# Down's sums kept running in PSUM, leftover feature tiles ahead of Down, and x split inside Down's last chunk

## The chip, the cores and the metric

The kernel runs on one core of a Trainium2 chip. A core has TensorE for matmuls (results go to PSUM, 8 banks of 128 partitions x 512 numbers), VectorE (DVE) and ScalarE (ACT) for elementwise work, GpSimd (POOL) for elementwise work in SBUF, and SyncE (SP), which here issues the DMAs in one queue. The metric is the device time of one execution in microseconds.

## The reference

One decoder layer on x of 1024 tokens x 1024 channels in f32, pre-norm with residual adds:

```python
x = x + (sigmoid(g_a) * y_a W_a + sigmoid(g_b) * y_b W_b) @ W_out   # mixers
h = rms_norm(x, norm_ffn)
x = x + (silu(h @ w_gate) * (h @ w_up)) @ w_down                    # D_FF = 2816
gate = sigmoid(rms_norm(x, norm_ple) @ w_pg)
x = x + gate * (p @ w_pp)
out = rms_norm(x, norm_final)
```

The change lies in the product with `w_down`, called Down here, and in the gate with `w_pg` behind it (the embedding gate).

## The kernel before

Everything is held transposed: x as 8 tiles `x2[m]` of 128 channels x 1024 tokens, two token halves of 512. A matmul takes a 128 x 128 weight block and a 128 x 512 operand. For f32 accuracy each number is split into a rounded part and a rest: `split` (L104 to 106) writes the rounded part with ScalarE and the rest with VectorE (`whi` and `wlo` for weights, `t` for operands), `split_gain` (L109, 110) does so with a gain (`xsh`, `xsl`); `mm3` (L85 to 87) then needs three matmuls per block.

**Gate and Up** (L818 to 838) go over 11 pairs of feature tiles, i = 0 to 10. Each pair is computed by Strassen's seven products (`strassen`), running on in PSUM: bank `x` takes products 1, 3, 5 and 7, bank `y` the 4th and 6th, and ScalarE copies partial sums out on the way (L685). The result `ys`, four blocks of 128 x 512 (two feature tiles by two halves), is turned by `stage` into Down's seven operands (`b11` to `t4`, four POOL subtractions), split, and written to DRAM (`d_o[i]`, 512 KB each) during the next pair's Gate. The last pair, i = 10, is the leftover: its four blocks go to DRAM as they are (`d_l`, L838).

**Down** is Strassen again: a chunk c takes four feature tiles (pairs 2c and 2c + 1), of which there are five, and each chunk goes over four pairs of output tiles, mp. For each (c, mp), seven products of six matmuls (`product`, two feature blocks by three), 140 in all. The order of all engines in this loop is that of the program, written by hand (`manual_schedule`, L894); work from outside may be put in between. Each product has a PSUM bank of its own. After the following product is issued, VectorE adds the bank onto one of seven targets (`evacuate`, L880): three are parts of x, four are sums in SBUF, `u1, u5, u6, u7`, which in chunk 0 are filled by ScalarE copies instead (L878). In the last chunk, when an mp is done, `combine` (L889) adds these sums onto x: eight adds of 128 x 512 for each mp, on POOL and partly on VectorE.

The weights of a step are two raw pieces of 256 KB (`wraw`, six buffers). `prepare` makes four sums of half pieces on POOL (L860 to 863) and splits them with four buffers of `whi` and `wlo`, one step ahead. The operands of chunk c + 1 are loaded from DRAM (L149) while chunk c runs, 14 loads of 512 KB through a ring of 24 buffers (8 `tap`, 12 `tbp`, 4 `spare`); those of chunk 0 during the last Up. In the last chunk `d_l` is loaded and split into `act`.

**The leftover** follows (L946 to 959): for each of 8 output tiles and two halves, six matmuls, then VectorE adds the bank to x (L956), x is split with its gain (L109, 110), and its square (ScalarE, L598) is added to `acc` by POOL (L599).

**The embedding gate** (L988 to 1000) then makes, for each m, 24 matmuls of `w_pg` with the split x for the first half; `stat` turns `acc` into 1 / rms with small matmuls (L116) and a chain of small VectorE operations (L119 to 129), `spread` spreads it over partitions, `finish` applies it, the sigmoid and the embedding, and adds squares for the last norm on VectorE (L599). The second half follows, and the output.

Apart from the hand-written loops a planner orders the instructions of each engine ahead of time, by program order and by when it reckons that inputs and buffers are ready; each engine then works its list in order, and so does SP. A buffer is given anew once the last reader of its old tile is done.

## Time and profile before

| | us |
|---|---|
| median of 3 runs | 1478.54 |
| lowest, highest | 1475.67, 1483.15 |
| the profiled execution | 1479.81 |
| its span | 1477.6 |
| TensorE busy | 1425.9 (96%) |
| VectorE busy | 1018.9 (69%) |
| ScalarE busy | 640.4 (43%) |
| POOL busy | 450.6 (30%) |

Busy time counts instructions as long as they are in the engine; matmuls overlap, so a busy TensorE isn't one at its peak. `PEclk` is the granted clock of TensorE as a share of full speed. Up ends and Down begins about 1132 us into the span; the leftover part ends at about 1352, the embedding gate's last matmuls at about 1460.

### The profile page before, as it was taken

How to read it: one execution, taken by the hardware profiler on the slowest of the kernel's cores; microseconds unless marked ns; L12 is line 12 of the kernel's file. 1: busy time of each engine (PE TensorE's matmuls, PEld its weight loads, DVE VectorE, ACT ScalarE, POOL GpSimd, SP SyncE). 2: the span in 40 equal slices, each digit the busy share in tenths (PEclk: the TensorE clock that was granted, in tenths of full speed). 3: DMA queues.
4: the chain of work that ended last, by engine and by line, in shares of the span. 5: the costliest groups of instructions: out<-in, count | busy, mean ns of one | idle time of the engine just before them, and what ended most of it. 6: DMA issues, size and time to landing. Idle time of an engine off the chain costs nothing.

```text
span 1477.6 us, 19192 instructions
## 1 busy us (share of the span) xinstructions
PE 1425.9 (96%) x6538; PEld 1171.9 (79%) x6538; DVE 1018.9 (69%) x1556; ACT 640.4 (43%) x1190; POOL 450.6 (30%) x491
## 2 busy tenths in 40 slices
PE   8999999999999999998899999999999999987995
PEld 6888888888888878885688888888887888875885
DVE  7681268888787776579666666666664476799786
ACT  6131455555555543345344444444443322225443
POOL 5000012232223200015444444444433233379001
PEclk9999999999999999999899999999999999998998
DMA  5141875555442177332244443444457766511452
GB/s 200 57 133 39 270 214 157 143 150 150 139 112 93 43 248 264 108 115 94 93 143 156 157 155 138 157 150 152 153 208 300 268 251 253 195 49 53 135 180 69
DMA packets 102673, 226.98 MB, mean 154 GB/s; under 512 B 10928, under 2 KB 22704, under 8 KB 102576
## 3 DMA queue, kind: packets, MB, share of 16 engines
q1 hardware_dynamic: 102576, 225.77, 46.0%
q8 instruction: 51, 0.84, 0.2%
q14 instruction: 46, 0.38, 0.1%
HBM read 154.42 MB, written 71.30 MB: 153 GB/s over the span
## 4 chain that ended last, share of the span: by engine, by line
PE 80%; DVE 10%; issue 6%; POOL 1%; DMA 1%; ACT 1%; SPq 0%; POOLq 0%; DVEq 0%; ACTq 0%
PE mm L87 25%; PE mm L86 25%; PE mm L85 25%; DVE wlo L106 2%; DVE fail L411 1%; PE pt L429 1%; DVE t L106 1%; DVE xsl L110 1%; PE av L445 1%; PE av L444 1%; PE z L401 1%; PE z L402 1%; DVE ev L606 1%; DVE x L956 1%; PE mm L141 1%
## 5 line engine op out<-in xcount | busy, mean ns | idle before, releaser
L85 PE MATMUL mm<-t,whi 128*128 128x512 f32 x960 | 381.2, 397 | 9.8 <-ACT t L105 4.4
L105 ACT CAST whi<-wraw 128x512 fp32r<-128x512 f32 x336 | 206.2, 620 | 412.2 <-PE mm L86 245.0
L87 PE MATMUL mm<-t,wlo 128*128 128x512 f32 x960 | 379.4, 396 | 4.3 <-DVE wlo L106 4.3
L106 DVE TENSOR_TENSOR wlo<-wraw,whi 128x512 fp32r<-128x512 f32 x336 | 253.6, 760 | 188.1 <-ACT whi L105 181.3
L86 PE MATMUL mm<-t,whi 128*128 128x512 f32 x960 | 379.5, 395 | 3.8 <-DVE t L106 3.8
L85 PEld LDWEIGHTS mm<-t,whi 128*128 128x128 f32 x960 | 182.0, 190 | 55.6 <-ACT t L105 6.0
L87 PEld LDWEIGHTS mm<-t,wlo 128*128 128x128 f32 x960 | 181.8, 189 | 47.1 <-DVE wlo L106 6.1
L86 PEld LDWEIGHTS mm<-t,whi 128*128 128x128 f32 x960 | 182.2, 190 | 46.2 <-DVE t L106 5.3
L85 PE MATMUL mm<-xs,whi 128*128 128x512 f32 x384 | 154.6, 403 | 0.0
L87 PE MATMUL mm<-xs,wlo 128*128 128x512 f32 x384 | 150.4, 392 | 0.0
L86 PE MATMUL mm<-xs,whi 128*128 128x512 f32 x384 | 150.2, 391 | 0.0
L106 DVE TENSOR_TENSOR t<-ev,t 128x512 fp32r<-128x512 f32 x98 | 96.9, 1010 | 32.9 <-ACT t L105 32.6
L694 POOL TENSOR_TENSOR ws<-wraw 128x512 f32<-128x512 f32 x22 | 29.8, 1353 | 286.4 <-DVE wlo L106 138.6
L411 DVE TENSOR_TENSOR_SCAN fail<-fail 128x1024 f32<-128x1024 f32 (+3 forms) x64 | 87.3, 1365 | 27.3 <-POOL fail L409 26.9
L105 ACT CAST t<-ev 128x512 fp32r<-128x512 f32 x102 | 61.6, 620 | 82.0 <-DVE ev L739 37.7
L409 POOL TENSOR_SCALAR_AFFINE_SELECT fail<-fail 128x128 f32<-128x128 f32 x64 | 20.6, 322 | 226.6 <-ACT fail L407 201.1
L105 ACT CAST ath<-pt 128x256 fp32r<-128x256 f32 (+1 forms) x176 | 54.8, 335 | 69.5 <-PE pt L429 38.8
L87 PEld LDWEIGHTS mm<-xs,wlo 128*128 128x128 f32 x384 | 72.1, 188 | 15.8
L85 PEld LDWEIGHTS mm<-xs,whi 128*128 128x128 f32 x384 | 72.2, 188 | 11.8 <-ACT sg L373 0.2
L86 PEld LDWEIGHTS mm<-xs,whi 128*128 128x128 f32 x384 | 72.3, 188 | 11.6
L106 DVE TENSOR_TENSOR atl<-pt,ath 128x256 fp32r<-128x256 f32 (+1 forms) x176 | 61.3, 367 | 18.2 <-ACT ath L105 17.8
L410 POOL TENSOR_SCALAR_AFFINE_SELECT beta<-beta 128x128 f32<-128x128 f32 x64 | 66.6, 1041 | 22.5 <-ACT beta L408 21.5
(187 smaller groups left out, 2570.1 us busy)
## 6 DMA issues: line engine op xcount, KB each, us to landing
d_t<-t SPq DMA_DIRECT2D x40, 512.0 KB, 3.3
t<-d_t SPq DMA_DIRECT2D x40, 512.0 KB, 5.9
d_b<-t SPq DMA_DIRECT2D x30, 512.0 KB, 2.7
t<-d_b SPq DMA_DIRECT2D x30, 512.0 KB, 7.3
wraw<-in_w_gate SPq DMA_DIRECT2D x44, 256.0 KB, 2.8
wraw<-in_w_up SPq DMA_DIRECT2D x44, 256.0 KB, 3.0
wraw<-in_w_down SPq DMA_DIRECT2D x44, 256.0 KB, 5.1
wraw<-in_w_out SPq DMA_DIRECT2D x32, 256.0 KB, 3.3
```

The lines of the kernel that those rows point to most:

```text
L85: nc.tensor.matmul(ps, w[0], x[0], start=first, stop=False, skip_group_check=onto)
L86: nc.tensor.matmul(ps, w[0], x[1], start=False, stop=False, skip_group_check=onto)
L87: nc.tensor.matmul(ps, w[1], x[0], start=False, stop=last, skip_group_check=onto)
L105: nc.scalar.copy(hi, src)
L106: (eng or nc.vector).tensor_sub(lo, src, hi)
L110: nc.vector.scalar_tensor_tensor(lo, src, g, hi, ALU.mult, ALU.subtract)
L141: nc.tensor.matmul(ps, ones, diag, start=True, stop=True)
L401: nc.tensor.matmul(zo, q[:, base:base + P], kh[:, ks], start=True, stop=False)
L409: nc.gpsimd.affine_select(r[:, :P], r[:, :P], [[1, P]], ALU.is_gt, 1.0, base=0, channel_multiplier=-1)
L410: nc.gpsimd.affine_select(b[:, :P], b[:, :P], [[1, P]], ALU.is_gt, 0.0, base=0, channel_multiplier=-1)
L411: nc.vector.tensor_tensor_scan(r[:, :w], r[:, :w], r[:, :w], 1.0, ALU.mult, ALU.bypass)
L694: nc.gpsimd.tensor_add(s1, a21, a22)
```

## The change

Down's seven products are reordered (`t3` before `b22`), so that four of them run on in a bank that already holds an earlier sum. Two steps (output pairs) form a unit of 14 products that alternate between the pairs; each pair has banks `x`, `z` and `y`, used in the order x z x y x y x. After each product, VectorE adds the bank's present contents straight onto the part of x that this partial sum belongs to (`target`); the sums in SBUF and `combine` are gone. `Weights` holds the parts of `prepare`, spread over the slots of the unit before.

The leftover is now pair i = 0: its four blocks are split and stored during the next Gate (`plain_store`), loaded during the last Up (`plain_loading`), and multiplied between Up and Down, ahead of the loop. Chunk c takes pairs 2c + 1 and 2c + 2. The operands of the last pair, i = 10, aren't stored: `keep` splits them into SBUF (`last`), and the last chunk uses them from there. The ring is replaced by a list of homes for each chunk.

In the last chunk, a part of x that has had all its sums is split with its gain by `final`, at most one in a slot, into tiles in the place of `tbp` and `spare`. The squares of x move behind the first gate matmuls, on VectorE (`squares`); the embedding gate takes the second half of the tokens first, and its first three results wait in PSUM for the statistics.

```diff
@@ constants, scratch, staging @@
-DOWN = ("b11", "b21", "t2", "t1", "b22", "t3", "t4")
+DOWN = ("b11", "b21", "t2", "t1", "t3", "b22", "t4")
-    d_o = [{n: scr(f"d_{n}{i}", [P, S]) for n in DOWN} for i in range(FT // 2 - 1)]
-    d_l = [[scr(f"d_l{e}{h}", [P, HALF]) for h in range(2)] for e in range(2)]
+    d_o = {i: {n: scr(f"d_{n}{i}", [P, S]) for n in DOWN} for i in range(1, FT // 2 - 1)}
+    d_l = [[scr(f"d_l{e}{h}", [P, S]) for h in range(2)] for e in range(2)]
-    def store(dst, src):
+    def to_dram(dst, src):
     ...
+    def stage(ys, store):
     ...
@@ loads of operands @@
-    ring = {"at": 20}
-
-    def ring_pair():
-        i = ring["at"] % 24
-        ring["at"] += 1
-        return pair_tile(tap if i < 8 else tbp if i < 20 else spare)
+    homes = {0: [tbp] * 6 + [spare] * 4 + [tap] * 4, 1: [tap] * 4 + [tbp] * 10,
+             2: [tbp] * 2 + [spare] * 4 + [tap] * 8, 3: [tbp] * 12 + [spare] * 2, 4: [tap] * 7}
     ...
+        home = iter(homes[c])
         for n in DOWN:
-            o[n] = []
-            for k in range(2):
-                t = ring_pair()
-                move(t, d_o[2 * c + k][n])
-                o[n].append(sides(t))
+            o.setdefault(n, [])
+            for i in (2 * c + 1, 2 * c + 2):
+                if i < NF - 1:
+                    t = pair_tile(next(home))
+                    move(t, d_o[i][n])
+                    o[n].append(sides(t))
+                    yield
+
+    def plain_store(ys):
+        for (e, h), y in ys.items():
+            to_dram(d_l[e][h], y)
+            yield
+
+    plain = [[], []]
+
+    def plain_loading():
+        for e in range(2):
+            for h in range(2):
+                t = pair_tile(tap)
+                move(t, d_l[e][h])
+                plain[e].append(sides(t))
                 yield
+    ops = loading(0, op)
     ...
-        if i == NF - 1:
-            ops = loading(0, op)
-            for _ in range(4):
-                next(ops)
         ys = {}
+        early = plain_loading()
         for n, _ in enumerate(strassen([w_up[2 * i], w_up[2 * i + 1]], up_out(ys))):
-            if i == NF - 1 and n in (2, 3, 4, 5, 6):
-                next(ops)
-                next(ops)
-        if i < NF - 1:
-            staging = stage(i, ys)
-        else:
-            for (e, h), t in ys.items():
-                nc.sync.dma_start(d_l[e][h], t)
+            if i == NF - 1 and n > 0:
+                for _ in range(2):
+                    next(early if n < 3 else ops)
+        if i == 0:
+            staging = plain_store(ys)
+        elif i < NF - 1:
+            staging = stage(ys, lambda n, y, d=d_o[i]: to_dram(d[n], y))
@@ Down: kept operands, weights, leftover part @@
+    tb3x = ctx.enter_context(ExitStack())
+    tb3 = tb3x.enter_context(pool("tb3"))
+    wsp = tb3x.enter_context(pool("wsp", 2))
+    last = {}
+
+    def keep(n, y):
+        t = tb3.tile([P, S], F32R, name=f"k{n}")
+        split(*sides(t), y)
+        last[n] = sides(t)
+
+    staging = stage(ys, keep)
+    units = [(c, mpp) for c in range(NC) for mpp in range(KT // 4)]
     q = HALF // 2
     ...
+    class Weights:
     ...
+        def sums(self):
+            self.sx, self.s1 = ev(), ev(q)
+            s2, s4 = (self.sx.rearrange("p (k e d) -> p e k d", e=2, d=P)[:, e] for e in range(2))
+            s1 = self.s1.rearrange("p (k d) -> p k d", d=P)
+            nc.gpsimd.tensor_add(s1, self.a21, self.a22)
+            nc.gpsimd.tensor_sub(s2, s1, self.a11)
+            nc.gpsimd.tensor_sub(self.a21, self.a11, self.a21)
+            nc.gpsimd.tensor_sub(s4, self.a12, s2)
+
+        def both(self, n, m, w):
+            self.w[n], self.w[m] = (w, (0, 2)), (w, (1, 3))
+
+        def w1(self):
+            self.both(0, 1, halves(self.x))
+
+        def w2(self):
+            self.both(2, 5, halves(self.sx))
+
+        def ws(self):
+            pair = tuple(wsp.tile([P, q], F32R, name=n) for n in ("wsh", "wsl"))
+            split(*pair, self.s1)
+            self.w[3] = pair, (0, 1)
+
+        def w3(self):
+            self.both(4, 6, halves(self.y))
+
+    def target(mp, n):
+
+        e, h = ((0, 0), (0, 0), (0, 1), (1, 1), (1, 1), (0, 1), (1, 0))[n]
+        return 2 * mp + e, h
+
+    pair = [Weights(0, 0), Weights(0, 1)]
+    for w in pair:
+        for e in range(2):
+            w.load(e)
+    for m2 in range(KT // 2):
+        raw = fp.tile([P, HALF], F32, name="wraw", bufs=NRAW)
+        nc.sync.dma_start(raw.rearrange("p (m n) -> p m n", m=2),
+                          w_down[2 * m2:2 * m2 + 2, :, :2 * P].rearrange("m p n -> p m n"))
+        w = halves(raw)
+        if m2 > 1:
+            pair[m2 - 2].sums()
+        for e in range(2):
+            for h in range(2):
+                ps = bank()
+                for k in range(2):
+                    mm3(ps, col(w, 2 * e + k), plain[k][h], k == 0, k == 1)
+                xx = x2[2 * m2 + e][:, hs(h)]
+                nc.vector.tensor_add(xx, ps, xx)
+            next(staging, None)
+            if m2 > 0:
+                next(ops, None)
+    run(staging)
+    run(ops)
+    for w in pair:
+        w.w1()
+    pair[0].w2()
+    xs3 = []
+    fresh = []
+
+    def final(m, h):
+        split_gain(*part(xs3[m], hs(h)), x2[m][:, hs(h)], gain(2, m))
+
@@ Down: the units @@
+        def evacuate():
+            m, h, ps, done = waiting
+            xx = x2[m][:, hs(h)]
+            nc.vector.tensor_add(xx, ps, xx)
+            if done:
+                fresh.append((m, h))
+
+        for u, (c, mpp) in enumerate(units):
     ...
+                    tbx.close()
+                    sparex.close()
+                    xsp = ctx.enter_context(pool("xsp", side="right"))
+                    xs3 += [(xsp.tile([P, S], F32R, name=f"xsh{m}"), xsp.tile([P, S], F32R, name=f"xsl{m}"))
+                            for m in range(KT)]
+            ahead = [Weights(units[u + 1][0], 2 * units[u + 1][1] + i) for i in range(2)] if u + 1 < len(units) else None
+            steps = {0: [pair[1].w2], 1: [pair[0].ws], 2: [pair[1].ws], 3: [pair[0].w3], 4: [pair[1].w3]}
+            if ahead:
+                a, b = ahead
+                loads = {0: [(a, 0), (a, 1)], 1: [(b, 0)], 6: [(b, 1)]}
+                steps |= {7: [a.sums], 9: [b.sums], 11: [a.w1], 12: [b.w1], 13: [a.w2]}
+            else:
+                loads = {}
+            banks = [{}, {}]
+            for slot in range(14):
+                n, i = divmod(slot, 2)
+                for w, e in loads.get(slot, ()):
+                    w.load(e)
+                w, cols = pair[i].w[n]
+                name = "xzxyxyx"[n]
+                x = op[DOWN[n]] + ([last[DOWN[n]]] if c == NC - 1 else [])
+                ps = banks[i][name] = product(w, x, cols, banks[i].get(name))
                 if waiting:
-                    evacuate(*waiting)
-                waiting = i, n, ps
-                if n % 2 == 1 and mp < 3 or mp == 3 and n >= 1:
+                    evacuate()
+                waiting = *target(2 * mpp + i, n), ps, c == NC - 1 and n not in (0, 2, 3)
+                for step in steps.get(slot, ()):
+                    step()
+                if c == NC - 1 and fresh:
+                    final(*fresh.pop(0))
+                if mpp == 0 and slot % 2 == 1 and slot < 12 or mpp == 1 and slot % 2 == 1 or mpp == 1 and slot in (4, 8):
                     next(ops, None)
     ...
-    for _ in combine(KT // 2 - 1):
-        pass
     ...
+            pair = ahead
+        evacuate()
+        for x in fresh:
+            final(*x)
+    tb3x.close()
+    tapx.close()
     ...
@@ the embedding gate @@
+    def squares(h):
+        for m in range(KT):
+            square_into(acc, m, hs(h), nc.vector)
+
+    def spread_into(inv, sl, dg):
+        nc.scalar.copy(inv[:, sl], spread(psp, dg, (sl.stop - sl.start) // P))
+
+
+    held = []
     for m in range(KT):
         w = pieces(w_pg[m])
-        got = ple_gate(m, w, hs(0))
+        held.append((m, *ple_gate(m, w, hs(1))))
         if m == 0:
-            dgs = [stat(psp, acc[:, hs(i)], 4, ev()) for i in range(2)]
-            held = got
-            continue
-        if m == 1:
-            for i in range(2):
-                nc.scalar.copy(inv3[:, hs(i)], spread(psp, dgs[i], 4))
-            finish(0, *held, hs(0))
-        finish(m, *got, hs(0))
+            squares(1)
+        elif m == 1:
+            dg = stat(psp, acc[:, hs(1)], 4, ev())
+            squares(0)
+        elif m == 2:
+            spread_into(inv3, hs(1), dg)
+            dg = stat(psp, acc[:, hs(0)], 4, ev())
+        elif m == 3:
+            spread_into(inv3, hs(0), dg)
+        while m > 1 and held:
+            finish(*held.pop(0), hs(1))
+
     ...
```

## Rows read from the trace of the kernel before

**Rows 1.** Head of the page: span and instructions.

```profile
span 1477.6 us, 19192 instructions
```

**Rows 2.** Stretches: length, PE, PEld, DVE, ACT, POOL busy (count), PEclk, DMA share, GB/s.

```profile
1050.00:1097.00 47.00, 47.00 (x206) 38.16 (x205) 31.09 (x40) 22.00 (x40) 21.16 (x15) 1.00 0.43 157
...
1180.00:1220.00 40.00, 40.00 (x177) 32.95 (x176) 28.09 (x47) 9.30 (x17) 11.83 (x16) 1.00 0.66 239
...
1350.00:1360.00 10.00, 5.82 (x26) 4.40 (x24) 10.00 (x13) 7.79 (x13) 10.00 (x7) 1.00 0.00 0
```

**Rows 3.** Waits of TensorE from 1050: total us, times, longest.

```profile
PE mm L87 <- DVE wlo L106: 13.8, 3, 9.7
```

**Rows 4.** TensorE's timeline, last Up product: start, duration, what, idle before.

```profile
1115.20 0.80 PE L85 MATMUL mm<-t,whi 128*128 128x512 f32 x1 [3.20 <-ACT ev L685]
...
1118.29 0.40 PE L86 MATMUL mm<-t,whi 128*128 128x512 f32 x1
```

**Rows 5.** TensorE's timeline at the end of Down.

```profile
1321.44 0.50 PE L87 MATMUL mm<-t,wlo 128*128 128x512 f32 x1 [0.40 <-DVE wlo L106]
...
1328.20 0.80 PE L87 MATMUL mm<-t,wlo 128*128 128x512 f32 x1 [3.72 <-DVE wlo L106]
...
1333.38 0.40 PE L87 MATMUL mm<-t,wlo 128*128 128x512 f32 x1
```

**Rows 6.** TensorE's timeline at the start of the embedding gate.

```profile
1365.52 0.80 PE L87 MATMUL mm<-xsh,wlo 128*128 128x512 f32 x1 [9.70 <-DVE wlo L106]
...
1369.52 0.63 PE L87 MATMUL mm<-xsh,wlo 128*128 128x512 f32 x1
1369.95 2.25 PE L116 MATMUL mm<-ones,acc 128*128 128x1 f32 x16
```

**Rows 7.** Groups of instructions from 1132 to 1365: count, busy us, mean ns, idle before.

```profile
L889 POOL TENSOR_TENSOR x<-x,s 128x512 f32<-128x512 f32 x15 | 23.3, 1565 | 3.0 <-DVE x L889 1.3 <-DVE x L880 1.2
...
L861 POOL TENSOR_TENSOR wraw<-wraw 128x256 f32<-128x256 f32 x19 | 14.7, 771 | 1.5
```

**Rows 8.** Tile x on VectorE, 1130 to 1365: ns min/median/max, first and last start.

```profile
L880 DVE TENSOR_TENSOR x<-mm,x x60: 674/681/685, 1135.0 to 1333.1; 128x512 f32<-128x512 f32 x60
L956 DVE TENSOR_TENSOR x<-mm,x x16: 675/678/683, 1334.8 to 1362.0; 128x512 f32<-128x512 f32 x16
L110 DVE SCALAR_TENSOR_TENSOR xsl<-x,g_sb,xsh x15: 750/1182/1778, 1336.3 to 1362.6; 128x512 fp32r<-128x512 f32 x15
```

**Rows 9.** VectorE's timeline, end of Down and first statistics.

```profile
1333.13 0.68 DVE L880 TENSOR_TENSOR x<-mm,x 128x512 f32<-128x512 f32 x1
...
1334.83 1.28 DVE L956 TENSOR_TENSOR x<-mm,x 128x512 f32<-128x512 f32 x2
...
1371.34 0.16 DVE L119 TENSOR_SCALAR nrm_a<-mm 128x4 f32<-128x4 f32 x1 [2.39 <-PE mm L116]
...
1376.30 0.87 DVE L129 TENSOR_SCALAR ev<-ident,nrm_y 128x128 f32<-128x128 f32 x4
```

**Rows 10.** Tile wlo on VectorE, 1130 to 1365: ns min/median/max.

```profile
L106 DVE TENSOR_TENSOR wlo<-wraw,whi x64: 681/693/1777, 1131.3 to 1363.7; 128x512 fp32r<-128x512 f32 x64
```

**Rows 11.** Timeline of SP's queue, last Up: start, us at it, DMA, count.

```profile
1097.73 3.09 SPq L149 DMA_DIRECT2D t<-d_b  x4
1100.87 0.67 SPq L535 DMA_DIRECT2D wraw<-in_w_up  x1
...
1118.57 11.32 SPq L838 DMA_DIRECT2D d_l<-ev  x3
```

**Rows 12.** Tile wraw on SP, 1130 to 1320: from issue to landing.

```profile
DMA to landing us min/median/max: 2.5/4.7/9.6
```

**Rows 13.** Group of the page: split of an operand on VectorE.

```profile
L106 DVE TENSOR_TENSOR t<-ev,t 128x512 fp32r<-128x512 f32 x98 | 96.9, 1010 | 32.9 <-ACT t L105 32.6
```

**Rows 14.** Tile acc, 1330 to 1470: squares added on VectorE, ns min/median/max.

```profile
L599 DVE TENSOR_TENSOR acc<-acc,ev x16: 418/684/693, 1385.7 to 1462.8; 128x512 f32<-128x512 f32 x12, 128x256 f32<-128x256 f32 x4
```

**Rows 15.** Stretch of the first gates, columns as in rows 2.

```profile
1378.00:1421.00 43.00, 43.00 (x192) 35.13 (x191) 32.48 (x54) 21.26 (x35) 0.00 (x0) 1.00 0.45 141
```

More of the change, by code (lines that the diff above doesn't have):

```diff
@@ L901, in hybrid_block @@
                 if c == NC - 1:
-                    act = [operand(tap, 2) for _ in range(2)]
-            if i + 1 < len(order):
-                ahead = prepare(raws.pop(i + 1))
-            for n, name in enumerate(DOWN):
-                if n == 0 and i + 2 < len(order):
-                    raws[i + 2] = load(i + 2)
-                if i + 1 < len(order) and n in (1, 2, 5, 6):
-                    w_next = next(ahead)
-                ps = product(w[n][0], op[name], w[n][1])
-                if waiting:
-                    evacuate(*waiting)
-                waiting = i, n, ps
-                if n % 2 == 1 and mp < 3 or mp == 3 and n >= 1:
-                    next(ops, None)
-                if c == NC - 1:
-                    if mp == 0:
-                        if n < 4:
-                            t = ev()
-                            nc.sync.dma_start(t, d_l[n // 2][n % 2])
-                            split(*act[n // 2][n % 2], t)
-                    else:
-                        if n == 0:
-                            comb = combine(mp - 1)
-                        next(comb, None)
@@ L926, in hybrid_block @@
-            for _ in comb:
-                pass
-            if c < NC - 1 and mp == 3:
+                    tbx.close()
[4 more added lines that the diff above has]
+            ahead = [Weights(units[u + 1][0], 2 * units[u + 1][1] + i) for i in range(2)] if u + 1 < len(units) else None
@@ L929, in hybrid_block @@
+            if c < NC - 1 and mpp == 1:
                 run(ops)
                 op = nxt
-            w = w_next
-        evacuate(*waiting)
-    for _ in combine(KT // 2 - 1):
-        pass
-    tbx.close()
-    sparex.close()
-    accx.close()
-    xsp = ctx.enter_context(pool("xsp", side="right"))
-    xs3 = [(xsp.tile([P, S], F32R, name=f"xsh{m}"), xsp.tile([P, S], F32R, name=f"xsl{m}")) for m in range(KT)]
+            pair = ahead
+        evacuate()
+        for x in fresh:
+            final(*x)
@@ L942, in hybrid_block @@
+    tb3x.close()
+    tapx.close()
     pp = ctx.enter_context(pool("ple"))
     acc = pp.tile([P, S], F32, name="acc")
-    for c in range(KT // 2):
-        raw = fp.tile([P, HALF], F32, name="wraw", bufs=NRAW)
-        nc.sync.dma_start(raw.rearrange("p (m n) -> p m n", m=2),
-                          w_down[2 * c:2 * c + 2, :, 4 * NC * P:].rearrange("m p n -> p m n"))
-        w = halves(raw)
-        for e in range(2):
-            for h in range(2):
-                m = 2 * c + e
-                ps = bank()
-                for k in range(2):
-                    mm3(ps, col(w, 2 * e + k), act[k][h], k == 0, k == 1)
-                xx = x2[m][:, hs(h)]
-                nc.vector.tensor_add(xx, ps, xx)
-                split_gain(*part(xs3[m], hs(h)), xx, gain(2, m))
-                square_into(acc, m, hs(h), nc.gpsimd)
```

90 lines of the change are left out of this document (27 added, 63 removed).

## The prediction

> **What bounds the kernel now.** The page's head gives the span, 1477.6 us [rows 1]; the execution it was taken from took 1479.8 us, 2.2 of them outside the span, and the median of the three runs, 1478.5, is 1.3 below it. I work against 1479.8 and subtract 1.3 at the end.
>
> I read the table by stretch first. In Up (1050 to 1097) and in mid Down (1180 to 1220) TensorE is busy all the time at the full clock; VectorE, in mid Down, 28.1 of 40 us: TensorE is the bound, with room on VectorE. From 1350 to 1360 that is turned round: VectorE and POOL 10.0 of 10.0, TensorE 5.8 [rows 2]. The waits of TensorE after 1050 then say what its idle time waited for: 13.8 us in 3 waits for `wlo`, a VectorE split, the longest 9.7 [rows 3]. TensorE's own timeline shows what each costs. A matmul follows the last after 0.23 us at the full clock, and after 0.43 for a while behind each long gap (the lower level of the clock).
> - Front, in the last Up product: 3.20 us idle; 7 matmuls then take 3.09 instead of 1.61, 1.5 lost: **4.7** [rows 4].
> - End of Down: 0.40 and 3.72 idle; 12 matmuls then take 5.2 instead of 2.8: **6.5** [rows 5].
> - Just inside the embedding gate: 9.70 idle; 9 matmuls then take 4.0 instead of 2.1: **11.6** [rows 6].
>
> Together 22.8 us of TensorE time in the stretch that the change rewrites.
>
> **The change part by part.**
>
> *TensorE's work* stays: 140 products of 6 matmuls and 96 for the leftover tiles in both versions. A product is 6 x 0.23 = 1.38 us, a unit of 14 products 19.3 us, the leftover part 22.1 us. So nothing is to be won in the middle of Down, only in the losses above.
>
> *Sums in PSUM.* 32 combining adds in the last chunk go: 23 on POOL (15 of them 1565 ns each [rows 7]), 9 on VectorE. ScalarE's 16 copies of the first chunk become VectorE adds, so VectorE has 140 evacuations instead of 124. One takes 681 ns, and they start 0.60 apart (two in 1.28) [rows 8, 9]. Per unit VectorE has 14 x 0.60, six full splits at about 0.61 and two half ones at 0.34: 12.8 of 19.3 us. The 16 new ones are among the 28 of the first chunk's two units, which keep 6.5 us free each: nothing. What replaces the separate banks is a wait: a product that runs on in a bank may not start until VectorE has read it. Queued behind the waiting matmul is all of TensorE. The two pairs put three products, 4.1 us, between a bank's end and its next use; VectorE needs 0.68 plus at most one split ahead of it, 1.78 at the longest [rows 10]. I take 0; it becomes a cost once VectorE runs more than 4.1 us late. It has done so: counted back from the gate's start at about 1352, the 96 leftover matmuls with 6.1 us lost among them began at about 1324, so the last Strassen product's evacuation, at 1333.13 [rows 9], was some 9 us late. That late in the new loop would be 5 us of waiting.
>
> *Leftover tiles first.* They leave the end, where each of the 16 results needed an evacuation, a gained split and mostly a POOL add, and go between Up and Down. What stalled the front goes with the order of loads: before, four 512 KB operand loads stand on SP at 1097.73, ahead of the next weights, and the stores of the last Up hold SP for 11.3 us further on [rows 11]. After, the Up weights come first, the operand loads start from the second product on, and those stores don't exist (the last stage's operands stay in SBUF), so the leftover part's weights can land during the last Up product: 4.7 us in the middle, 9.6 at most [rows 12]. I take the front's 4.7 as gone. What is late next there is VectorE: 16 evacuations (9.6), four splits of weights and three for the first unit (7 x 1.1, between the median and the longest of [rows 10], as POOL works beside them) and seven kept splits at 0.99 [rows 13] are 24.2 us against 22.1. Least cost 0, since the kept splits have until the last chunk; most, at 1.78 for all 14 splits, 34.5 - 22.1 = 12.4, and 2.0 for the clock behind it (as in the bullets), 14.4. I take 2.1, by the middle of the rows.
>
> *x split in the last chunk.* 16 gained splits move from behind Down into its last two units. They took 1182 ns in the median, with POOL at work, and 750 at the least [rows 8]; 0.67 apart in the second case, with the same 0.08 of overlap as above. In the first of the two units (POOL adds weights in it, 8 x 0.77 [rows 7]) VectorE has 14 evacuations, 8 splits of x, six full and two half splits of weights. At the slow durations that is 8.4 + 9.4 + 6.6 + 1.0 = 25.4, 6.1 over the 19.3, and 8.1 with the clock; at the fast ones 8.4 + 5.4 + 3.7 + 0.7 = 18.2, no stall. In the second unit POOL has no work: 8.4 + 5.4 + 2.5 + 1.2 for the gate's first weights = 17.5. I take 1.0, near the fast end, as POOL works only 6 us of the 38.6. The evacuations are 674 to 685 ns throughout [rows 8], a split with both inputs in SBUF 681 to 1777 [rows 10].
>
> The Trainium skill ("SBUF — State Buffer", Who interferes with whom) states that a VectorE instruction with two SBUF inputs contends with a GpSimd instruction that reads SBUF, and that one with at most one such input does not. By that rule the second unit has no slow split, and the chunk costs what 6 us of POOL cause, about 1 us; without it, by the median of the old splits, 8.1. The trace agrees: the evacuations don't vary, the splits do.
>
> *The gate after Down.* TensorE can go on at once, since the gate's first half needs nothing of the last product. What moves there is the sum of squares: 14 adds, from POOL at the end of Down to VectorE between the gates (684 ns, 0.60 apart: 8.4 us) [rows 14]. From 1378 to 1421 VectorE was busy 32.5 of 43.0 us [rows 15]; for the eight gates of 44 us that is 33.3. With two statistics of together 5.9 us (1371.34 to 1377.2 [rows 9]) it is 33.3 + 8.4 + 5.9 = 47.6, against TensorE's 44 and 2.3 of small matmuls [rows 6]. The squares stand ahead of the splits of the next weights, which TensorE waits for. Least 0; most the 8.4 in full with 2.0 of clock, 10.4. I take 3.0: the 1.3 of excess, and as much again since it comes in the first gates. The results held back occupy three of eight banks, which costs nothing.
>
> *Loads.* As many chunk loads of 512 KB less seven, into chosen homes. I walked each: the tightest are those of the sixth operand, issued behind products 7 and 8 of a chunk's second unit into tiles last read by its products 0 and 1. Over 8 us lie between: 0.
>
> Sum: 22.8 - 2.1 - 1.0 - 3.0 = 16.7. 1479.8 - 16.7 - 1.3 = 1461.8, forecast **1462** (1457 to 1468 for errors of the three costs).
>
> **The rivals.**
> - *All is hidden*: the three costs are 0: 1479.8 - 22.8 - 1.3 = 1455.7. For it: 0.40 us of waiting left the clock alone [rows 5], and most waits have slack. Against: VectorE's sums come out over the limit in two places.
> - *VectorE stays the bound at the end*: the last chunk at its 8.1 and half of the gate's 10.4: 22.8 - 2.1 - 8.1 - 5.2 = 7.4 gained, 1471. For it: the 10.0 of 10.0 there now, and that the work is the same but for the adds. Against: POOL, which stretched the splits, is nearly idle in the new end.
> - *The stall moves to the start of Down*: the front at its 14.4, the rest as forecast: 22.8 - 14.4 - 4.0 = 4.4, 1474. The leftover part would be as VectorE-bound in its new place as in the old.
> - *SP is held by an operand load* (slower): a load whose home tile is still read stops the weight loads queued behind it on SP, as the stores held it for 11.3 us [rows 11]. The last weight of a unit is issued at product 6 and its sum is split at 14: 11.0 us, of which landing takes 4.7 and POOL's four adds 3.1, so 3.2 are spare; 8.1 late and 2.0 of clock are 10.1 for each such chunk. From three of the four chunk changes on it outweighs the gain: 1492 to 1502. Against it is the walk above.
> - *Waits one by one* (the change doesn't do what it says): each of the 80 products that run on in a bank waits 0.1 us for its evacuation: 8 us, 1470. Against it: Gate and Up run on in PSUM too, with one other product between, and mid Up shows none [rows 2].
>
> The Trainium skill ("PSUM — Partial Sum Buffer", PSUM bank collisions raise a hardware error) asks that a bank be guarded by semaphore whatever address in it is read. By that the wait is there for each of those products and none can be left out; it would give 1470 if VectorE just misses each, and the forecast if it is never late. Mid Up, guarded in the same way, agrees with the second.
>
> **How the numbers follow.** Forecast 0.56, all hidden 0.13, VectorE-bound end 0.16, front 0.06, SP held 0.05, one by one 0.04. A measurement of this kernel can tell about 0.5% from no change, 7.4 us: faster ends at 1471.1, slower begins at 1485.9. Faster: 0.56 + 0.13 + half of 0.16 + 0.01 of the front + 0.02 of the waits = 0.80. Slower: the 0.05 of SP. Same: 0.15. The range takes in 1455.7 and the two waits' cases, with 2.7 below for the estimate of the losses: 1453 to 1473; outside lie SP, the upper part of the front and of the VectorE case, and a little below, some 0.16.
>
> **What would show it.** Right: no wait of 3 us on TensorE between 1097 and the end of Down; the leftover's matmuls directly behind Up; evacuations at 0.68; splits of x at 0.75 in the last unit; the gate's first matmuls within 1 us of the last product, and its start some 15 to 20 us earlier. Wrong: waits of TensorE for an evacuation of x inside Down (bank), for `wlo` in the first unit (front) or in gates 2 to 6 (squares), or SP entries of many us in Down. A time above 1473 means that VectorE or SP took the place of the stall; one below 1453, that I missed a loss.

## The result, and the profile after

The changed kernel takes 1468.68 us in the median of six runs (1465.48 to 1471.42), the kernel before 1483.26 beside it (1475.67 to 1484.08): a ratio of 0.991, 95% interval 0.9892 to 0.9928, so 10.7 to 16.0 us faster. On another chip, later, it was 0.9897 (0.9875 to 0.9918). The forecast was 1462, worked out from a kernel before at 1478.5, the median of its first three runs. Against the 16.7 us of its sum the gain is real and some 2 to 5 us short: 14.6 between the medians, 11.6 between the two profiled executions, 1479.81 and 1468.20, in which the terms can be followed.

Head of the page, then stretches (PE, PEld, DVE, ACT and POOL busy, PEclk, DMA share, GB/s), of the kernel after:

```profile
span 1466.5 us, 19073 instructions
```

```profile
1110.00:1120.00 10.00, 10.00 (x45) 8.20 (x44) 3.39 (x5) 2.94 (x5) 2.59 (x3) 1.00 1.01 388
1120.00:1130.00 10.00, 7.00 (x30) 5.09 (x29) 7.30 (x9) 2.18 (x4) 5.29 (x5) 1.00 0.77 292
1130.00:1140.00 10.00, 10.00 (x39) 7.96 (x38) 9.94 (x13) 4.04 (x7) 4.67 (x4) 0.83 0.56 185
1160.00:1200.00 40.00, 40.00 (x175) 32.50 (x173) 28.88 (x45) 8.70 (x16) 12.36 (x18) 1.00 0.66 247
...
1330.00:1340.00 10.00, 8.41 (x36) 6.26 (x35) 9.42 (x17) 3.81 (x7) 0.00 (x0) 1.00 0.17 52
...
1350.00:1360.00 10.00, 9.63 (x47) 7.84 (x46) 9.52 (x17) 6.34 (x12) 0.00 (x0) 1.00 0.50 173
1360.00:1370.00 10.00, 7.55 (x32) 5.72 (x32) 8.47 (x24) 4.33 (x9) 0.00 (x0) 0.95 0.14 45
1370.00:1380.00 10.00, 10.00 (x32) 7.78 (x33) 6.38 (x22) 4.00 (x6) 0.00 (x0) 0.71 0.21 63
```

The middle of Down is as it was: TensorE 40.00 of 40, VectorE 28.88 (28.09 in [rows 2]). What differs is at three seams, and each has a smaller wait where a larger one was, or one where none was. Waits of TensorE after, from 1050 (total us, times, longest), against the 13.8 us for `wlo` of [rows 3]:

```profile
PE mm L141 <- DVE ev L129: 5.8, 3, 4.9
PE mm L116 <- DVE acc L600: 5.3, 3, 2.5
PE mm L87 <- DVE wlo L106: 1.8, 1, 1.8
PE mm L85 <- DVE x L949: 1.6, 2, 1.2
PE mm L85 <- ACT whi L105: 1.2, 1, 1.2
```

L949 is the evacuation inside Down (L880 before), L600 the add of a square. The 4.9 (4.7 before) and one 2.5 belong to the end of the kernel and are in both versions.

**Front.** TensorE's timeline (start, duration, what, idle before):

```profile
1126.07 0.50 PE L85 MATMUL mm<-t,whi 128*128 128x512 f32 x1 [1.23 <-ACT whi L105]
...
1129.05 0.50 PE L87 MATMUL mm<-t,wlo 128*128 128x512 f32 x1 [1.78 <-DVE wlo L106]
```

Behind the second wait the matmuls come 0.43 apart instead of 0.23 until 1133.5, with the granted clock at 0.83 in that slice. Why the weights are late is seen on SP (start, us at it, DMA, count) and in the landing of its `wraw` loads, 1095 to 1125:

```profile
1107.26 0.33 SPq L535 DMA_DIRECT2D wraw<-in_w_down  x1
1107.69 1.81 SPq L149 DMA_DIRECT2D t<-d_l  x4
1111.79 2.43 SPq L149 DMA_DIRECT2D t<-d_b  x4
1114.51 1.00 SPq L149 DMA_DIRECT2D t<-d_t  x2
1115.60 0.38 SPq L535 DMA_DIRECT2D wraw<-in_w_down  x1
1116.14 1.67 SPq L917 DMA_DIRECT2D wraw<-in_w_down  x2
```

```profile
DMA to landing us min/median/max: 2.6/6.2/9.1
```

The leftover's first weights (L917) are issued at 1116.14, behind ten operand loads of 512 KB (5.2 MB, 13.5 us at the 388 GB/s of 1110 to 1120). With 9.1 us to landing that is 1125.2, when Up's last matmuls are done (TensorE is idle until 1126.07). ScalarE and VectorE (timelines of each) then show a second queue:

```profile
1124.88 0.62 ACT L105 CAST kb<-ev 128x512 fp32r<-128x512 f32 x1 [7.01 <-PE mm L87]
1125.40 0.61 ACT L105 CAST whi<-wraw 128x512 fp32r<-128x512 f32 x1
```

```profile
1125.49 2.38 DVE L106 TENSOR_TENSOR kb<-ev,kb 128x512 fp32r<-128x512 f32 x2
1127.79 1.21 DVE L106 TENSOR_TENSOR wlo<-wraw,whi 128x512 fp32r<-128x512 f32 x1
```

Two kept splits (`kb`) stand ahead of the weights' rest `wlo` in VectorE's list. The first wait, for `whi`, is thus mostly the late landing; the second, for `wlo`, has these two splits in it as well.

**End of Down.** TensorE, with the gate's first matmul last:

```profile
1332.81 0.47 PE L85 MATMUL mm<-t,whi 128*128 128x512 f32 x1 [1.22 <-DVE x L949]
...
1338.97 0.47 PE L85 MATMUL mm<-t,whi 128*128 128x512 f32 x1 [0.37 <-DVE x L949]
...
1347.41 0.39 PE L85 MATMUL mm<-xsh,whi 128*128 128x512 f32 x1
```

Evacuations over Down and splits of `x` on VectorE (ns min/median/max), against [rows 8], and VectorE's timeline ahead of the longer wait:

```profile
L949 DVE TENSOR_TENSOR x<-mm,x x138: 676/692/693, 1153.7 to 1348.0; 128x512 f32<-128x512 f32 x138
...
L110 DVE SCALAR_TENSOR_TENSOR xsl<-x,g_sb,xsh x13: 739/752/753, 1312.4 to 1347.3; 128x512 fp32r<-128x512 f32 x13
its engine sat idle before it (us, times) until:
...
  ACT xsh L109: 3.8, 10
```

```profile
1331.31 0.75 DVE L110 SCALAR_TENSOR_TENSOR xsl<-x,g_sb,xsh 128x512 fp32r<-128x512 f32 x1 [0.19 <-ACT xsh L109]
1331.98 0.68 DVE L949 TENSOR_TENSOR x<-mm,x 128x512 f32<-128x512 f32 x1
```

The bank comes free when the evacuation of 1331.98 ends. VectorE reached it late, having waited ten times, 3.8 us in all, for ScalarE's rounded part `xsh` of the split just ahead: seven times about 0.2 us, and 0.79 in each of three where nothing stood between the evacuation and the split of the same part.

**Gate.** TensorE, then VectorE:

```profile
1368.83 1.76 PE L116 MATMUL mm<-ones,acc 128*128 128x1 f32 x8 [2.45 <-DVE acc L600]
1370.45 0.77 PE L85 MATMUL mm<-xsh,whi 128*128 128x512 f32 x1
```

```profile
1362.90 4.67 DVE L600 TENSOR_TENSOR acc<-acc,ev 128x512 f32<-128x512 f32 x6
1367.49 0.68 DVE L106 TENSOR_TENSOR wlo<-wraw,whi 128x512 fp32r<-128x512 f32 x1
1368.09 0.68 DVE L600 TENSOR_TENSOR acc<-acc,ev 128x512 f32<-128x512 f32 x1
```

The first half's statistics stand in TensorE's list ahead of the fourth result and wait for the last square; the 12 matmuls behind come 0.43 apart.

**The ledger.** From TensorE's timeline I sum, over each stretch, how far the distance between starts goes beyond 0.23 us per matmul. The gate's column holds some 2.8 us of small matmuls and short gaps that every version keeps.

| us lost | front | end of Down | first gates |
|---|---|---|---|
| before | 4.8 | 7.0 | 13.0 |
| after | 5.1 | 2.1 | 7.8 |
| after, second chip | 3.9 | 2.0 | 6.9 |

That is 24.8 before and 15.0 after: 9.8 of the 11.6 us. Some 0.9 of the rest is there before 1085 us, in code that the change doesn't touch, and 0.5 lies outside the two spans, which are 11.1 apart. The gate's column is the least exact: from the gate's first matmul to the spread of the last norm's first half (L141 at 1424.54 before, 1413.64 after) it is 72.1 us before and 66.2 after, 5.9 less where the ledger has 5.2; and by the same count the changed kernel takes 64.7 on the second chip. Differences of under some 1.5 us in this column, between executions on different chips, tell nothing.

What went is thus the end of Down and part of the gate; the front's loss has only changed its cause. No run separates the leftover's move from the sums in PSUM.

### The profile page after: what moved, and what is told of

It is laid out like the page before. It is cut to its first block, busy times and chain, and to the rows that moved or that the text cites. A ratio compares the mean times of both kernels' runs of the same rounds, so it can differ in the third digit from the quotient of the medians.

```text
span 1466.5 us, 19073 instructions
## 1 busy us (share of the span) xinstructions
PE 1424.5 (97%) x6538; PEld 1170.6 (80%) x6538; DVE 1021.8 (70%) x1577; ACT 630.6 (43%) x1174; POOL 393.2 (27%) x454
## 4 chain that ended last, share of the span: by engine, by line
PE 82%; DVE 8%; issue 6%; DMA 1%; POOL 1%; ACT 1%; SPq 0%; DVEq 0%; POOLq 0%; ACTq 0%
PE mm L87 25%; PE mm L86 25%; PE mm L85 25%; DVE fail L411 1%; PE pt L429 1%; DVE t L106 1%; DMA xt<-in_xT 1%; DVE wlo L106 1%; PE av L445 1%; PE av L444 1%; PE z L401 1%; PE z L402 1%; DVE ev L607 1%; PE mm L116 0%; PE mm L141 0%
## 5 line engine op out<-in xcount | busy, mean ns | idle before, releaser
L85 PE MATMUL mm<-t,whi 128*128 128x512 f32 x896 | 354.8, 396 | 9.1 <-ACT t L105 4.1
L105 ACT CAST whi<-wraw 128x512 fp32r<-128x512 f32 x316 | 193.8, 620 | 388.3 <-PE mm L86 264.6
L86 PE MATMUL mm<-t,whi 128*128 128x512 f32 x896 | 353.6, 395 | 4.1 <-DVE t L106 4.1
L87 PE MATMUL mm<-t,wlo 128*128 128x512 f32 x896 | 353.3, 395 | 2.0 <-DVE wlo L106 2.0
L106 DVE TENSOR_TENSOR wlo<-wraw,whi 128x512 fp32r<-128x512 f32 x316 | 233.5, 744 | 125.3 <-ACT whi L105 124.2
L85 PEld LDWEIGHTS mm<-t,whi 128*128 128x128 f32 x896 | 169.2, 189 | 53.0 <-ACT t L105 6.0
L86 PEld LDWEIGHTS mm<-t,whi 128*128 128x128 f32 x896 | 169.2, 189 | 43.6 <-DVE t L106 5.6
L87 PEld LDWEIGHTS mm<-t,wlo 128*128 128x128 f32 x896 | 169.1, 189 | 41.1 <-DVE wlo L106 2.8
L949 DVE TENSOR_TENSOR x<-mm,x 128x512 f32<-128x512 f32 x140 | 96.1, 690 | 42.8 <-PE mm L87 39.4
L106 DVE TENSOR_TENSOR t<-ev,t 128x512 fp32r<-128x512 f32 x91 | 89.9, 1010 | 30.7 <-ACT t L105 30.3
L105 ACT CAST t<-ev 128x512 fp32r<-128x512 f32 x95 | 57.5, 620 | 81.7 <-DVE ev L740 42.2
L87 PEld LDWEIGHTS mm<-xs,wlo 128*128 128x128 f32 x384 | 72.1, 188 | 15.7
```

The lines of the kernel that those rows point to most:

```text
L85: nc.tensor.matmul(ps, w[0], x[0], start=first, stop=False, skip_group_check=onto)
L86: nc.tensor.matmul(ps, w[0], x[1], start=False, stop=False, skip_group_check=onto)
L87: nc.tensor.matmul(ps, w[1], x[0], start=False, stop=last, skip_group_check=onto)
L105: nc.scalar.copy(hi, src)
L106: (eng or nc.vector).tensor_sub(lo, src, hi)
L949: nc.vector.tensor_add(xx, ps, xx)
```

## The experiments

All start from the changed kernel; ratios are to the kernel before on the same chip. "Lost" is the ledger's sum for the column named.

**Front: kept splits, or late weights?** `keep_late`: the kept splits and the loads of the leftover part start a step later.

```diff
-            next(staging, None)
             if m2 > 0:
+                next(staging, None)
                 next(ops, None)
```

> The kept splits of the last Up begin one step later, behind the leftover part's first two output tiles. Theory A: at the start of the leftover part the kept splits stand in ScalarE's and VectorE's lists ahead of the split of the leftover weights (ScalarE casts kb at 1124.88, the weights at 1125.40; VectorE does two kb of 1.2 us before wlo), and this is TensorE's wait of 1.23 and 1.78 us with 2.0 us of slow clock behind it: the waits go and the time falls by 4 to 5 us, to about 1464. Rival B: the leftover weights land late, since ten operand loads of 512 KB go ahead of them on SP: the wait stays at 2 us or more and the time changes by less than 1.5 us.

0.9908 (0.9881 to 0.9934); 4.1 us lost in front. The edit did not move what it was to move. The planner orders these lists itself, and VectorE still makes two kept splits ahead of `wlo`:

```profile
1126.55 1.82 DVE L106 TENSOR_TENSOR kb<-ev,kb 128x512 fp32r<-128x512 f32 x2
1128.29 1.22 DVE L106 TENSOR_TENSOR wlo<-wraw,whi 128x512 fp32r<-128x512 f32 x1
```

What TensorE waits for in front, 2.1 us for `whi` in one piece, is what it waits for in `after_again`, the unchanged kernel. So this run is no test of the kept splits. It does show the late landing, for here ScalarE waits for the DMA itself:

```profile
1127.33 0.62 ACT L105 CAST whi<-wraw 128x512 fp32r<-128x512 f32 x1 [0.76 <-DMA wraw<-in_w_down]
```

`loads_late`: from the fourth product of the last Up on, one operand load a step instead of two, and the rest two a step in the leftover part.

```diff
-                for _ in range(2):
+                for _ in range(2 if n < 3 else 1):
                     next(early if n < 3 else ops)
...
             if m2 > 0:
+                next(ops, None)
                 next(ops, None)
```

> Only 4 instead of 8 operand loads of chunk 0 are issued in the last Up; the other 10 come in the leftover part, two at a time. Rival B (leftover weights land late behind operand loads): the waits at the start of the leftover part go, 4 to 5 us less, about 1464. Theory A (kept splits ahead in the lists): the waits of 1.23 and 1.78 us stay within 0.5 us, time unchanged within 1.5 us. If operands of chunk 0 are then late, TensorE waits at the start of Down instead, for a DMA.

0.9889 (0.9868 to 0.9911); 0.7 us lost in front. Two things differ here: counted from the request of the last Up weights, the leftover's are requested 1.1 us sooner (18.3 us behind it instead of 19.4, and again 9.1 to landing), and the planner now puts their splits ahead of the last kept ones. The run can't tell the two apart.

`weights_first`: the leftover's first two pieces are requested ahead of the first unit's four (`leftover(m2)` makes the load that stood in the loop).

```diff
     ...
+    raws = [leftover(0), leftover(1)]
     pair = [Weights(0, 0), Weights(0, 1)]
...
-        raw = fp.tile([P, HALF], F32, name="wraw", bufs=NRAW)
     ...
-        w = halves(raw)
+        w = halves(raws.pop(0) if raws else leftover(m2))
```

> The first two pieces of leftover weights are requested ahead of the four pieces for the first unit, so they take the two buffers that are free at about 1099, before the operand loads. If the stall at the start of the leftover part is their late landing (thinning the operand loads took it from 3.0 to 0.5 us, delaying the kept splits only to 2.1), it is gone: no wait over 0.5 us between 1110 and 1140, full clock there, about 5 us less than the changed kernel, 1463 to 1464. Rival: VectorE's sum in the leftover part (24.2 us of work for 22.1) makes the wait come back as one for wlo at the next weights or at the first unit: less than 2 us gained.

0.9864 (0.9847 to 0.9881); nothing lost in front. Its stretches:

```profile
1120.00:1130.00 10.00, 10.00 (x45) 8.12 (x44) 6.98 (x10) 2.38 (x4) 3.86 (x5) 1.00 1.04 402
1130.00:1140.00 10.00, 10.00 (x44) 8.03 (x44) 6.12 (x8) 3.03 (x6) 9.24 (x8) 1.00 0.39 138
```

TensorE is full at the full clock where it had 7.00 of 10 and then 0.83, with the DMA engines as busy as before. VectorE goes from two kept splits (1126.90) straight to an evacuation (1129.25): the weights have been split by then. So the place of two small loads behind the large ones is enough to make the front's loss, and their request ahead of them to take it away; 16 evacuations, weights' splits and kept splits do fit beside the leftover's matmuls. That the late landing alone makes a loss is seen in `after_again`: ScalarE waits 0.78 us for the DMA there, nothing waits for `wlo`, and 3.9 us are lost. What the kept splits add in the execution above, with its 1.78 us for `wlo`, is not shown, since no run moves them alone.

**End of Down.** `split_behind`: no split of x in the loop, all 16 behind Down.

```diff
-                if c == NC - 1 and fresh:
-                    final(*fresh.pop(0))
```

> The 16 gained splits of x are taken out of the last chunk and done behind Down. Theory: they are worth what VectorE then needs at the gate's start, with TensorE idle: 16 x 0.67 = 10.7 us and about 2 us of slow clock, less the 1.6 us of bank waits in the last chunk: 10 to 12 us slower than the changed kernel, 1479 to 1481, little under before. Rival: the gain of the change is the vanished combining adds, and the splits would be hidden anyway by ScalarE and VectorE running ahead of the gate's matmuls (which need them one by one): under 5 us slower.

0.9945 (0.9926 to 0.9965). The end of Down loses nothing, the gate 15.5 instead of 7.8; with the front's 4.5 the ledger is 5.0 us worse, as the two profiled times are (1473.09, 1468.20). Having the splits inside Down is worth 5, less than the 10 to 12 of the expectation and near its rival's "under 5". The rival's reason is seen in the trace: the gate takes its parts one by one, and TensorE's waits at its start are for the first weights (2.6 us) and for two single splits (1.2), not for all 16.

`pool_busy`: 24 adds on POOL that nothing needs, spread over the last chunk.

```diff
+            if c == NC - 1 and mpp == 0:
+                idle = pair_tile(tap).bitcast(F32)
+                nc.gpsimd.memset(idle, 0.0)
     ...
+                if c == NC - 1 and 1 < slot:
+                    nc.gpsimd.tensor_add(idle[:, :HALF], idle[:, HALF:], idle[:, HALF:])
```

> 24 idle adds of 128x512 on POOL (nobody uses their result) are put into the last chunk, from the second slot of each unit: about as much POOL work as the combining adds were there. Theory: splits with two SBUF inputs go from 0.68 and 0.75 to 1.1 to 1.8 us, evacuations stay at 0.68, VectorE falls behind and TensorE waits for evacuations (bank) in the last chunk: 1.6 us of such waits become 5 to 10, time 5 to 10 us more than the changed kernel. Rival: POOL beside VectorE is no matter here, only VectorE's own number of adds was: less than 1.5 us.

0.9942 (0.9925 to 0.9959), by the ratios 4.7 us slower than the changed kernel; 6.4 us lost at the end of Down instead of 2.1. Evacuations and splits, 1300 to 1350, on VectorE, and TensorE's wait:

```profile
L949 DVE TENSOR_TENSOR x<-mm,x x30: 673/679/693, 1300.3 to 1347.7; 128x512 f32<-128x512 f32 x30
L110 DVE SCALAR_TENSOR_TENSOR xsl<-x,g_sb,xsh x12: 751/1187/1504, 1312.8 to 1349.4; 128x512 fp32r<-128x512 f32 x12
```

```profile
PE mm L85 <- DVE x L949: 3.9, 1, 3.9
```

The median mixes two kinds: of the eight splits beside POOL adds seven took 1.17 to 1.50 us and one 0.75; the later ones, with POOL idle, 0.74 to 0.75. So with POOL at work the splits are back at durations like the 1182 of [rows 8], and the evacuations stay: the durations of before were POOL's doing, and having no POOL work beside the splits is what lets them fit.

`split_lag`: a part of x is split one slot later, so that ScalarE's half of it is begun a slot ahead of need.

```diff
+                due = len(fresh)
                 if waiting:
                     evacuate()
...
-                if c == NC - 1 and fresh:
+                if due:
```

> In the last chunk the gained split of a part of x is put one slot later in the lists, so that ScalarE's half of it is done while VectorE makes the next evacuation. Theory: the waits of TensorE for evacuations in the last chunk (1.2 and 0.4 us) come from VectorE idling behind ScalarE (ten waits, 3.8 us in all); they go, 1.5 us gained and not more. Rival: they come from VectorE's sum of work, and stay.

0.9889 (0.9871 to 0.9907). The bank waits are gone, and so is VectorE's idling for `xsh`. The time alone doesn't show the 1.5 us: the interval overlaps that of the changed kernel (0.9892 to 0.9928). The stretch against the 8.41 above:

```profile
1330.00:1340.00 10.00, 10.00 (x44) 8.10 (x44) 10.00 (x19) 4.47 (x8) 0.00 (x0) 1.00 0.18 52
```

**Gate: the place of the squares, or VectorE's work?** `squares_late`: the first half's squares at the fifth result instead of the second, their statistics at the seventh, the spread at the eighth.

```diff
-            squares(0)
         elif m == 2:
             spread_into(inv3, hs(1), dg)
+        elif m == 4:
+            squares(0)
+        elif m == 6:
             dg = stat(psp, acc[:, hs(0)], 4, ev())
-        elif m == 3:
+        elif m == 7:
             spread_into(inv3, hs(0), dg)
```

> The squares of the first token half move from gate 1 to gate 4, their statistics from gate 2 to gate 6. Theory: TensorE's list has these statistics' matmuls ahead of gate 3, so it stands 2.45 us (1366.4 to 1368.8) until VectorE has added seven squares, and 12 matmuls behind it run at the low clock: about 5 us less, 1464; no wait for acc over 0.5 us in the gates. Rival: VectorE's sum of work in the first gates is the limit (47.6 against 46.3 us), so that the wait comes back as one for wlo two or three gates later: less than 2 us gained.

0.9918 (0.9889 to 0.9946); 8.0 us lost in the gate, 7.8 in the changed kernel: nothing gained, as the rival had it. The 2.45 is gone from its place; TensorE waits 27 us later instead, not for `wlo` as the rival had it, but for the spread of these statistics:

```profile
1395.76 1.12 PE L141 MATMUL mm<-ev,ones 128*128 128x512 f32 x2 [2.82 <-DVE ev L129]
```

`squares_pool`: they go to POOL, statistics at the fifth result, spread at the seventh.

```diff
-            square_into(acc, m, hs(h), nc.vector)
+            square_into(acc, m, hs(h), nc.gpsimd if h == 0 else nc.vector)
     ...
+        elif m == 4:
             dg = stat(psp, acc[:, hs(0)], 4, ev())
-        elif m == 3:
+        elif m == 6:
             spread_into(inv3, hs(0), dg)
```

> The squares of the first token half are added by POOL (idle there) and their statistics come two gates later. Theory: VectorE's sum in the gates is the limit, so 4.2 us less of it takes the wait of 2.45 us and the slow clock behind it away, and none comes back: 4 to 6 us gained, about 1463. Rival: the adds on POOL slow VectorE's two-input instructions beside them as they did before (0.68 to 1.1 and more), so that VectorE gains nothing and the waits stay within 1 us of what they are.

0.9908 (0.9892 to 0.9923); 9.4 us lost. POOL takes 1295 ns for each add (tile `acc`), and TensorE waits 3.96 us in one piece, at 1370.53, for the spread of the other half's statistics. The rival's reason holds: beside POOL's adds VectorE's chain of small operations for these takes from 1361.01 to 1370.47, 9.5 us, where the changed kernel takes from 1359.94 to 1362.99, about 3. Every other of its operations is held up, to as much as 1.15 us instead of 0.16, and the four of L129 take 2.77 instead of 0.88:

```profile
L600 POOL TENSOR_TENSOR acc<-acc,ev x7: 1267/1295/1322, 1360.7 to 1368.9; 128x512 f32<-128x512 f32 x7
```

```profile
1362.20 1.15 DVE L124 SCALAR_TENSOR_TENSOR nrm_t<-nrm_t,nrm_y 128x4 f32<-128x4 f32 x1
...
1367.70 2.77 DVE L129 TENSOR_SCALAR ev<-ident,nrm_y 128x128 f32<-128x128 f32 x4
```

`sq0_out`: seven of the eight squares of the first half are left out (it is the norm ahead of the embedding gate that lacks them, not the output's).

```diff
-        for m in range(KT):
+        for m in range(KT if h else 1):
```

> The changed kernel without seven of the eight squares of the first half (the output's norm is therefore not that of the reference): 7 VectorE adds of 0.60 us, 4.2 us, and 7 ScalarE squares less, nothing else changed. Theory (VectorE's sum in the gate is the limit): the wait for acc of 2.5 us and the slow matmuls behind it go, 4 to 6 us less than the changed kernel. Rival (the statistics' chain of small operations makes the wait, whatever the squares take): less than 2 us gained, and a wait of 2 us or more for acc or for the small operations stays within 1360 to 1375.

0.9882 (0.9865 to 0.99), beside `after_again` at 0.9897 on that chip: 1464.26 against 1466.45 us. The gate loses 2.8 instead of 6.9, 4.1 less, at the low end of the 4 to 6 expected; the front lost 5.8 against 3.9 in the profiled executions, which would leave the 2.2 that the medians show. In time that is under the theory's figure and just over the rival's "less than 2"; the trace decides for the theory. At the place of the 2.45:

```profile
1367.61 0.95 PE L116 MATMUL mm<-ones,acc 128*128 128x1 f32 x8
1368.41 0.48 PE L85 MATMUL mm<-xsh,whi 128*128 128x512 f32 x1
```

No wait, and the full clock behind. So what the gate loses beyond the 2.8 is these 4.2 us of VectorE work, which found no free place in the two positions run on VectorE, nor on POOL, where they hold up VectorE: each time something on TensorE's path waits. What was not tried is a longer way between statistics and spread in the late version.

**Together.** `wf_lag` is `weights_first` with `split_lag`; `wf_lag_late` has the later squares too; `after_again` is the changed kernel beside them. Their edits are those above.

> The changed kernel once more, beside the three others on one chip: a ratio to the kernel before of 0.991, as measured already, with TensorE waits of about 1.2 and 1.8 us in the leftover part, 1.2 and 0.4 for evacuations at the end of Down, and about 2.5 for acc in the gate.

> The leftover's weights requested first, and the split of a finished part of x one slot later. Theory (two separate causes on TensorE's path): the front's 5.0 us and the bank waits' 1.9 us both go, 6.9 us less than the changed kernel, about 0.0045 of ratio below it, and the trace shows no TensorE wait over 0.4 us from 1100 to the gate's second result. Rival (what is saved ahead of the gate is waited for in the gate, since VectorE is as late there as before): only about 5 us less, and the wait for acc in the gate grows by about 1.9 us, to over 4.

> As the one before, and the first half's squares and statistics three gates later. Theory (VectorE's work in the gate is more than TensorE's, so a move inside it gains nothing): within 1.5 us of the version without the later squares, with the wait for acc gone from the third gate and as much waiting in the later ones. Rival (it is only the place of the squares, right behind Down's backlog): the gate's 6 us go too, 4 to 6 us below that version.

| | median us | ratio (95%) | lost: front, end of Down, gate |
|---|---|---|---|
| after_again | 1466.45 | 0.9897 (0.9875 to 0.9918) | 3.9, 2.0, 6.9 |
| wf_lag | 1460.90 | 0.9860 (0.9842 to 0.9877) | 0, 0, 6.9 |
| wf_lag_late | 1462.87 | 0.9872 (0.9854 to 0.9890) | 0, 0, 9.1 |

The two causes are separate and add up: 5.9 us in the ledger, 5.5 in the medians. The rival's price of 5 is nearer than the theory's 6.9, but its reason fails: the gate loses 6.9 in both, the wait for `acc` being 2.94 in one piece instead of 0.35 and 2.47. (Of the 6.9 expected, 1 is the front, which lost less on this chip.) With the front and the end of Down free, `wf_lag` is the best version run by its median ratio (the interval of `weights_first` overlaps its own), 21.6 us below the kernel before in the medians of that chip. The later squares cost 2 us more. In `after_again` the front came otherwise than expected: one wait of 2.1 us for `whi` instead of two of 1.2 and 1.8.

## Why the prediction was right and where it was wrong

**Right.** The bound and the place of the gain: TensorE's work stays, the middle of Down gains nothing, the time comes out of the seams. No wait of 3 us stands between 1097 and Down's end (longest 1.78), and the gate's first matmul follows Down by 0.23 us. Evacuations at 0.68 and splits at 0.75 came out as taken; `pool_busy` shows why. What the Trainium skill says in "SBUF — State Buffer" (Who interferes with whom) held for these two: seven of the eight splits beside a POOL add, whose tensor inputs both lie in SBUF, take 1.17 to 1.50 us instead of 0.75, and the evacuations, with one, stay at 0.68. But one such input is no safeguard for every instruction: in `squares_pool` L121, whose one tensor input lies in SBUF, took 0.77 us beside a POOL add, and 0.17 in the changed kernel.

**Wrong, the front.** The step that failed is "so the leftover part's weights can land during the last Up product ... I take the front's 4.7 as gone". It took the 4.7 us to landing in the middle of [rows 12], where 9.6 stood in the same row. I had noted that the operand loads start "from the second product on" and didn't put the leftover's weights into that list: ten loads of 512 KB stand ahead of them, they are issued at 1116.14, and with 9.1 us to landing come as Up ends. The leftover's matmuls, which were to follow directly behind Up, wait 1.23 and 1.78 us. The price came out as 5.1 us, against the 2.1 of VectorE's sum; and that sum was no cost: with the weights in time the front loses nothing. How much of the 5.1 the two kept splits ahead of `wlo` add stays open.

**Wrong, the bank wait at 0.** The sum for the last chunk counted VectorE's own durations. A split that follows its evacuation also holds VectorE until ScalarE has made `xsh`, 0.2 us in seven cases and 0.79 in three: 3.8 us. Predicted for the chunk 1.0, measured 2.1; `split_lag` removes it by order alone.

**Wrong in size and form, the gate.** Predicted 3.0, as a wait for `wlo` behind the squares; measured 7.8, some 5 without the share that `sq0_out` keeps. The waiting instruction is the statistics' own matmul, which the change puts ahead of the fourth result. The prediction's sum over eight gates (47.6 against 46.3) was right that VectorE is over, but the excess falls on the first three gates, whole, and the 12 slow matmuls behind a wait of 2.45 cost 2.4 more.

**The rivals.** Of the 16.7 the ledger finds 9.8, 6.9 less: 3.0 more is lost in front, 1.1 in the last chunk and 2.0 in the gate (4.8 less the 2.8 that every version keeps), and the losses of before, counted without these 2.8, come out 0.8 lower. All three costs were thus too small, and the time still lies in the range because that reached to 1473. Two rivals name times nearer to the 1468.68 than the forecast is, the waits one by one (1470) and the VectorE-bound end (1471), but the kernel before came out at 1483.26 instead of 1478.5: by the gain, 14.6 us between the medians, the forecast's 16.7 is the nearest, and the 11.6 between the profiled executions lie about midway between it and the 7.4 of the VectorE-bound end. Of that rival the half in the gate came, 5.0 us without the 2.8 against its 5.2; the half in the last chunk did not, 2.1 instead of 8.1. The waits one by one did not come: mid Down has none. SP's entries of many us in Down, named as a sign against, are there (10.9 to 11.4 us in seven units, and one of 19.5), and no TensorE wait goes with them: the sign was no sign. "Its start some 15 to 20 us earlier" was wrong by the prediction's own terms: before the gate stood only the 4.7 and 6.5 lost; the start moved from 1352.44 to 1347.41.

## What to carry to other kernels

When a stage is moved, write down the whole list of its DMA queue, sizes included, and place the first small load in it; behind bulk loads take the longest landing time of the row, not its middle. In an engine's sum, count the handovers inside an instruction pair (ScalarE's rounded part, VectorE's rest) as well as the durations, and give the other engine a slot's lead. Where a planner orders the lists, read from the trace that an edit moved what it was to move before reading anything from its time. Work that was moved off a full stretch and still has to be done next to it comes back at the next point where an in-order engine needs its result.

## What the runs showed of the hardware

The clock did not follow from the length of one wait. The single 1.22 us at the end of Down left it full (1.00 in that slice), while in `sq0_out` waits of 1.43 and 1.06 us, 2.3 us from start to start, were followed by this slice, at 0.74:

```profile
1130.00:1140.00 10.00, 10.00 (x35) 7.96 (x34) 9.96 (x13) 4.04 (x7) 5.97 (x4) 0.74 0.55 185
```

Behind 2.45 us came 12 matmuls at 0.43 us. The same program lost 5.1 us in the front in one execution and 3.9 in another, with the DMA engines' share at 1.01 in the first (1110 to 1120); where weights land just as they are needed, the front is part of the run-to-run spread.
